# Root of the latents' mean squares on ScalarE (logarithm, exponential) instead of two POOL instructions

## The chip, the cores and the metric

One core of one Trainium2 chip runs the kernel. The metric is the time of one execution on the device in microseconds (us). A profiled execution gives the trace; there the engines are called PE (matrix multiply; its weight loads are PEld), DVE (vector), ACT (ScalarE, activation functions), POOL (GpSimd) and SP (DMA issue).

## The reference, cut to what matters

The reference is a trunk of two layers over 1024 tokens of width 1024. Each layer normalises the input, projects it, runs four branches A to D side by side, gates each, and projects the concatenation back. The change sits in branch D, the latent attention. Its queries and keys come from two normalised latents:

```
def rms_norm(x, g, eps=NORM_EPS):
    y = xf * lax.rsqrt(jnp.mean(jnp.square(xf), axis=-1, keepdims=True) + eps)
q  = (rms_norm(cq,  qa_g)  @ qb_w)     # cq: 256 wide
kv = (rms_norm(ckv, kva_g) @ kvb_w)    # ckv: 128 wide
```

Per token two factors are needed, 1/sqrt(mean(cq^2) + eps) and 1/sqrt(mean(ckv^2) + eps). Branch A, at work at the same time, ends in layer norm, SiLU and a pointwise matrix.

## The kernel before, in words

The tokens are cut into 8 tiles of 128, taken from tile 7 down to tile 0. Each stage of a layer is a Python generator: `th_a` to `th_atail` for branch A, `th_b`, `th_c`, `th_d` and `keys` for the latents, `th_att` for the attention itself, `th_w` for the loads of the output weights, `gate_f` for the gates. `weave` draws from them by the due times in `PLAN`, and this gives a program order. Tile's planner (`schedule_with_timeline_sim=True`, L1183) then orders each engine's queue with a timeline of its own: of the instructions of an engine that are ready in it, the one that stands first in the program goes first. So a queue need not follow the program, and at run time each engine takes its queue strictly in order.

Per tile, `th_d` multiplies by the split weights into `psd` (L209 to L211, 24 matmuls), copies the 384 latents to `cn` (ACT, L824), squares and sums them on ACT (`jd`, L827 and L828, with the sums in `ms`, 128x2), takes the root (L829), makes the queries' factor `rq` (DVE, L830), transposes `cn` on PE (L832) and copies the parts out (`ckT`, `cqT`). `keys`, one tile later, multiplies `ckT` (`pk`, L847), scales it by `ms` on ACT (`kk` and `vD`, L850 and L851), transposes (L860) and copies into `kT`. `psd`, `pk` and the attention's `psc` share two PSUM buffers.

There are two helpers for the root. `rstd_p` (L145) uses two POOL instructions, an addition of eps (L146) and a power of -0.5 (L147); it is used for A, B, C and D. `rstd` (L141) uses two on ACT: a logarithm with eps as bias (L142) and an exponential with scale -0.5 (L143); it is used for the norms of the residual stream.

ACT evaluates a function only with its table in place. `pin_tables` (L1089) runs after the planner and puts a load of the one table that has both Exp and Ln ahead of an Exp or Ln where the last function from a table was another (L1103); loads for Silu and Sigmoid are put in ahead of the instruction that needs them and carry its line. Copy and Square need no load of their own. In the stretch of the latents, Exp comes from branch C (`lm`, L738) and from the attention (`pe`, L933), and Silu from the gates (L353) and from branch A (`hsA`, L507): two `hsA` instructions (m = 0 and 1) for each half of the tokens, whose input `pt2A` are transposes on PE (L506), and whose output is used by the pointwise matmuls `pyA` (L515).

Of the kernel before, what the change touches and what calls it, by code (L numbers as in the profile page):

```python
# [99 lines left out]
def trunk_kernel(ctx, tc, x, pos, pre_g, post_g, wd, wv, w256, wo, cols, rows, pw, qb, kvb,  # L100
# [11 lines left out]
    def big(name):  # L112
        return pbig.tile([P, 1024], F32, tag="big", name=name)
# [27 lines left out]
    def rstd(out_, ms, e=0):  # L141
        A.activation(out_, ms, AF.Ln, bias=eps[:, e:e + 1])  # L142
        A.activation(out_, out_, AF.Exp, scale=-0.5)  # L143

    def rstd_p(out_, ms, e=0):  # L145
        G.tensor_tensor(out_, ms, eps[:, e:e + 1].to_broadcast(list(ms.shape)), op=ALU.add)  # L146
        G.tensor_tensor(out_, out_, mhalf.to_broadcast(list(ms.shape)), op=ALU.pow)  # L147
# [11 lines left out]
    def copy(name, out_, in_):  # L159
        (V.tensor_copy if name in ONV else A.copy)(out_, in_)  # L160
# [17 lines left out]
    def load_chunk(l, which, idx=0, spare=None):  # L178

        hs, ls = [], []  # L180
        if which == "d":
            parts, kk, n = 4, 2, ND
        elif which == "v":
            parts, kk, n = 2, 4, NV
        else:
            parts, kk, n = 2, 4, 256
        for q in range(parts):
            src = wd[l, q] if which == "d" else wv[l, q] if which == "v" else w256[l, idx, q]
            raw = wst.tile([P, kk, n], F32, tag="raw", name="raw", bufs=NRAW)
            nc.sync.dma_start(out=raw, in_=src)  # L190
            if spare is not None and q == parts - 1:
                h = spare.tile([P, kk, n], F32R, tag="k4", name="wh4", bufs=NK4)
                lo = spare.tile([P, kk, n], F32R, tag="k4", name="wl4", bufs=NK4)
            else:
                h = wst.tile([P, kk, n], F32R, tag="wh", name="wh", bufs=NWH)
                lo = wst.tile([P, kk, n], F32R, tag="wl", name="wl", bufs=NWL)
            split("wh", h, lo, raw)
            for k in range(kk):
                hs.append(h[:, k, :])
                ls.append(lo[:, k, :])  # L200
        return hs, ls

    def proj_tok(hT, hs, ls, i, n, ps):

        hh, hl = hT
        for k in range(KD):
            a = hh[:, k, i * P:(i + 1) * P]
            b = hl[:, k, i * P:(i + 1) * P]
            T.matmul(ps[:, :n], a, hs[k], start=(k == 0), stop=False)  # L209
            T.matmul(ps[:, :n], a, ls[k], start=False, stop=False)  # L210
            T.matmul(ps[:, :n], b, hs[k], start=False, stop=(k == KD - 1))  # L211
# [67 lines left out]
    for l in range(L):  # L279
# [16 lines left out]
        def blk(name, n=512, shape=None, parts=P):  # L296
            return shaped(br.tile([parts, n], F32, tag="blk", name=name, bufs=NBLK, padded_shape=[P, 544]), shape)
# [4 lines left out]
        def tmp(n, name, shape=None, parts=P):  # L302
            tag, cap, nb = ("t1k", 256, NT1) if n <= 256 else ("t15", 384, NT15) if n <= 384 else ("t2k", 512, NT2)
            return shaped(br.tile([parts, n], F32, tag=tag, name=name, bufs=nb, padded_shape=[P, cap]), shape)

        def small(n, name, bufs=2, shape=None):
            return shaped(br.tile([P, n], F32, tag=name, name=name, bufs=bufs), shape)
# [489 lines left out]
        def th_d():  # L797
            nc.gpsimd.dma_start(out=qbt, in_=qb[l])
            nc.gpsimd.dma_start(out=kvt, in_=kvb[l])
            for kb in range(2):  # L800
                V.tensor_scalar(qbt[:, kb, :], qbt[:, kb, :], col[:, C_QAG + kb:C_QAG + kb + 1], None, op0=ALU.mult)
            V.tensor_scalar(kvt, kvt, col[:, C_KVG:C_KVG + 1], None, op0=ALU.mult)
            hs, ls = load_chunk(l, "d", spare=br)
            vts, behind = {}, None
            for i in ORDER:
                g = i // 4
                if (0, g) not in kT:
                    for h in range(4):
                        kT[h, g] = blk("kT", parts=100)

                        nc.gpsimd.dma_start(out=kT[h, g][96:100, :], in_=amask[0])
                    for c in range(2):
                        cqT[c, g] = blk("cqT")
                if i // 2 not in vts:
                    vts[i // 2] = blk("vD", 512, (P, 8, 64))
                vD[i] = vts[i // 2][:, (i % 2) * 4:(i % 2) * 4 + 4, :]
                csl = slice((i % 4) * P, (i % 4 + 1) * P)
                pd_ = big("psd")
                ps, pt = pd_[:, 0:512], pd_[:, 512:1024]
                proj_tok(hT, hs, ls, i, ND, ps)  # L820
                ms = small(2, "msd", 3)
                cn = tmp(384, "cn")
                jd = br.tile([P, 384], BF16, tag="jd", name="jd", bufs=1)
                copy("cn", cn, ps[:, 0:384])  # L824
                krd = small(32, "krd", 3, (P, 2, 16))
                copy("krd", krd.rearrange("p a j -> p (a j)"), ps[:, 384:416])
                A.activation(jd[:, 0:256], cn[:, 0:256], AF.Square, scale=1.0 / 16, accum_out=ms[:, 0:1])  # L827
                A.activation(jd[:, 256:384], cn[:, 256:384], AF.Square, scale=128.0 ** -0.5, accum_out=ms[:, 1:2])  # L828
                rstd_p(ms, ms)  # L829
                V.tensor_scalar(rq[:, i:i + 1], ms[:, 0:1], SCALE, None, op0=ALU.mult)  # L830
                for c in range(3):
                    T.transpose(pt[:, c * P:(c + 1) * P], cn[:, c * P:(c + 1) * P], idn)  # L832
                ckT = small(P, "ckT", 3)
                copy("ckT", ckT, pt[:, 256:384])
                for c in range(2):
                    copy(f"cqT{c}", cqT[c, g][:, csl], pt[:, c * P:(c + 1) * P])
                yield 6
                if behind is not None:
                    yield from keys(*behind)
                behind = (i, ckT, ms, krd)  # L840
            yield from keys(*behind)

        def keys(i, ckT, ms, krd):
            g, csl = i // 4, slice((i % 4) * P, (i % 4 + 1) * P)
            pk_ = big("pk")
            pk, ptk = pk_[:, 0:512], pk_[:, 512:1024]
            T.matmul(pk, ckT, kvt, start=True, stop=True)  # L847
            pkv = pk.rearrange("p (h d) -> p h d", h=4)
            kk = tmp(384, "kk", (P, 4, 96))
            scaled("kk", kk[:, :, 0:64], pkv[:, :, 0:64], ms[:, 1:2])  # L850
            scaled("vD", vD[i], pkv[:, :, 64:128], ms[:, 1:2])  # L851
            k1, k2 = small(32, "kr1", 2, (P, 2, 16)), small(32, "kr2", 2, (P, 2, 16))
            V.tensor_tensor(k1, krd, cosT[:, i], op=ALU.mult)
            for a in range(2):
                V.tensor_tensor(k2[:, a, :], krd[:, 1 - a, :], sinT[:, i, a, :], op=ALU.mult)
            V.tensor_tensor(k1, k1, k2, op=ALU.add)
            V.tensor_copy(kk[:, :, 64:96],
                          k1.rearrange("p a j -> p (a j)").unsqueeze(1).to_broadcast([P, 4, 32]))
            for h in range(4):
                T.transpose(ptk[0:96, h * P:(h + 1) * P], kk[:, h, :], idn)  # L860
            for h in range(4):
                copy(f"kT{h}", kT[h, g][0:96, csl], ptk[0:96, h * P:(h + 1) * P])
            yield 3
# [160 lines left out]
        def plan(name):  # L1024
# [5 lines left out]
            (islice(conv, plan("ca")[2]), plan("ca")), (conv, plan("cb")), (gate(7, 1), plan("gb")), (th_b(), plan("b")),  # L1030
            (gate_f(8, 0), plan("ga")), (gate_f(9, 1), plan("gd")), (gate(10, 2), plan("gc")),
            (th_x(), plan("x")), *([(th_rot(), plan("rot"))] if l == 0 else []), (th_atail(), plan("at")), (th_c(), plan("c")), (th_d(), plan("d")),
            (th_q0(), plan("q")))]
        weave(ths, plan("d")[1] + 0.5)
# [154 lines left out]
```

## Time and profile before

| | us |
|---|---|
| median of 3 runs (lowest to highest) | 1258.37 (1258.11 to 1260.59) |
| profiled execution, its own time | 1256.95 |
| its span, first to last instruction | 1255.2 |
| PE busy | 1196.8 (95% of the span) |
| DVE busy | 808.7 (64%) |
| ACT busy | 488.5 (39%) |
| POOL busy | 180.0 (14%) |

A busy PE is one with a matmul under way. An engine's busy time leaves out the issue of DMAs and semaphores. A row of a timeline gives an instruction's start, its duration, engine, line, operation, output and input, count, and in brackets the idle time before it and what ended that.

### The profile page before, as it was taken

To read this page: it belongs to the slowest core of one execution; us is meant where nothing else is said; L and a number is where in the kernel's file an instruction comes from. 1 tells how busy PE (TensorE), PEld (TensorE's weight loads), DVE (VectorE), ACT (ScalarE), POOL (GpSimd) and SP (SyncE) were. 2 spreads that over 40 slices of the span, in tenths; PEclk is the share of its full clock that TensorE was granted. 3 is DMA by queue.
4 is the path that set the end of the run, shared out by engine and by line. 5 is a ranking of instruction groups with operands and counts; after the bars stand their busy time and mean duration, and the time that the engine had idled before them with its cause. 6 is when DMAs were issued, how large, how long until landed. Compare 5 with 4: busy or idle time off the path is not lost.

```text
span 1255.2 us, 17851 instructions
## 1 busy us (share of the span) xinstructions
PE 1196.8 (95%) x6902; PEld 985.2 (78%) x6902; DVE 808.7 (64%) x1555; ACT 488.5 (39%) x1112; POOL 180.0 (14%) x290
## 2 busy tenths in 40 slices
PE   5999999999989989999999999998999898999997
PEld 5988899888878846677898889897888696567786
DVE  5566999985366575527454859999763775654432
ACT  5413222233456474425432222322344755643311
POOL 2100011101132111211020001211011232011100
PEclk9999999999989999999999999998999999999999
DMA  8002122211142140234321111211013312111532
GB/s 275 34 34 68 43 85 79 71 41 52 54 134 74 40 154 19 73 125 168 104 94 68 34 51 60 86 59 67 34 49 101 118 60 100 49 40 43 176 138 81
DMA packets 38661, 101.48 MB, mean 81 GB/s; under 512 B 5440, under 2 KB 13808, under 8 KB 38576
## 3 DMA queue, kind: packets, MB, share of 16 engines
q1 hardware_dynamic: 22848, 51.42, 12.1%
q0 software_dynamic: 14864, 46.04, 11.0%
q10 hardware_dynamic: 864, 2.88, 0.6%
q8 instruction: 54, 0.88, 0.3%
q14 instruction: 31, 0.25, 0.1%
HBM read 75.37 MB, written 25.20 MB: 80 GB/s over the span
## 4 chain that ended last, share of the span: by engine, by line
PE 76%; DVE 11%; issue 4%; DMA 4%; ACT 3%; POOL 0%; SPq 0%; DVEq 0%; ACTq 0%; POOLq 0%
PE pz L1012 11%; PE psx L220 4%; PE psx L223 4%; PE psx L226 4%; DVE ca L481 3%; PE poD L949 3%; PE psc L926 3%; PE ptp L944 2%; PE plB L625 2%; PE psA L220 2%; PE psA L223 2%; PE psA L226 2%; PE psgA L347 2%; PE psgA L348 2%; PE psgA L349 2%
## 5 line engine op out<-in xcount | busy, mean ns | idle before, releaser
L481 DVE SCALAR_TENSOR_TENSOR ca<-hpad,col,ca 128x512 f32<-128x512 f32 x240 | 186.1, 781 | 4.0
L176 DVE TENSOR_TENSOR wl<-raw,wh 128x1024 fp32r<-128x1024 f32 (+2 forms) x56 | 66.9, 1194 | 95.3 <-ACT wh L160 95.2
L160 ACT CAST wh<-raw 128x1024 fp32r<-128x1024 f32 (+2 forms) x56 | 57.5, 1027 | 141.5 <-PE psA L223 33.7
L1012 PE MATMUL pz<-woh,yh 128*128 128x512 f32 x240 | 76.9, 400 | 1.2 <-ACT yh L160 1.2
L1012 PE MATMUL pz<-woh,yl 128*128 128x512 f32 x240 | 76.6, 398 | 0.2 <-DVE yl L176 0.2
L1012 PE MATMUL pz<-wol,yh 128*128 128x512 f32 x240 | 76.0, 396 | 0.0
L209 PE MATMUL psg<-wh,hh 128*128 128x256 f32 x256 | 73.9, 289 | 1.5 <-ACT gt L160 1.4
L210 PE MATMUL psg<-wl,hh 128*128 128x256 f32 x256 | 73.2, 286 | 0.0
L211 PE MATMUL psg<-wh,hl 128*128 128x256 f32 x256 | 72.8, 284 | 0.0
L625 PE MATMUL plB<-qz,krb 128*128 128x128 f32 x448 | 62.8, 288 | 8.6 <-DVE krb L635 8.6
L625 PEld LDWEIGHTS plB<-qz,krb 128*128 128x128 f32 x448 | 58.0, 199 | 11.0 <-issue 5.1
L933 ACT ACTIVATE pe<-psc,nm 128x1024 f32<-128x1024 f32 (+7 forms) x64 | 47.1, 738 | 42.6 <-DVE nm L928 22.4
L220 PE MATMUL psx<-hh,wh 128*128 128x512 f32 x192 | 62.8, 406 | 0.0
L223 PE MATMUL psx<-hl,wh 128*128 128x512 f32 x192 | 62.2, 403 | 0.0
L226 PE MATMUL psx<-hh,wl 128*128 128x512 f32 x192 | 61.9, 401 | 0.0
L719 DVE SCALAR_TENSOR_TENSOR xbc<-xpad,col,xbc 128x512 f32<-128x512 f32 x72 | 51.1, 748 | 16.3 <-ACT xbc L172 15.5
L926 PE MATMUL psc<-kT,qTt 96*128 96x512 f32 (+4 forms) x128 | 53.4, 544 | 5.7 <-ACT pe L933 3.5
L1012 PEld LDWEIGHTS pz<-wol,yh 128*128 128x128 f32 x240 | 44.9, 188 | 10.3
L1012 PEld LDWEIGHTS pz<-woh,yl 128*128 128x128 f32 x240 | 44.7, 188 | 10.4 <-DVE yl L176 0.6
L1012 PEld LDWEIGHTS pz<-woh,yh 128*128 128x128 f32 x240 | 44.1, 188 | 10.7 <-ACT yh L160 1.4
L348 PE MATMUL psgA<-hl,wh 128*128 128x512 f32 x128 | 51.0, 398 | 0.0
L347 PE MATMUL psgA<-hh,wh 128*128 128x512 f32 x128 | 50.9, 397 | 0.0
(335 smaller groups left out, 3001.2 us busy)
## 6 DMA issues: line engine op xcount, KB each, us to landing
raw<-in_w_dram SPq DMA_DIRECT2D x44, 512.0 KB, 3.4
rawo<-in_wo_dram SPq DMA_DIRECT2D x16, 512.0 KB, 3.5
gsp<-gt POOLq DMA_DIRECT2D x16, 256.0 KB, 2.5
gl<-gsp POOLq DMA_DIRECT2D x8, 512.0 KB, 5.1
gspF<-gtA POOLq DMA_DIRECT2D x16, 256.0 KB, 2.3
ysp<-gl POOLq DMA_DIRECT2D x8, 512.0 KB, 3.4
lm<-acsp POOLq DMA_DIRECT2D x16, 256.0 KB, 4.0
yt<-ysp SPq DMA_DIRECT2D x16, 256.0 KB, 3.4
```

What stands on the lines that cost most here:

```text
L209: T.matmul(ps[:, :n], a, hs[k], start=(k == 0), stop=False)
L210: T.matmul(ps[:, :n], a, ls[k], start=False, stop=False)
L211: T.matmul(ps[:, :n], b, hs[k], start=False, stop=(k == KD - 1))
L220: T.matmul(ps[:, h * 512:(h + 1) * 512], w, hh[:, k, h * 512:(h + 1) * 512], start=(k == 0), stop=False)
L223: T.matmul(ps[:, h * 512:(h + 1) * 512], w, hl[:, k, h * 512:(h + 1) * 512], start=False, stop=False)
L226: T.matmul(ps[:, h * 512:(h + 1) * 512], wl, hh[:, k, h * 512:(h + 1) * 512], start=False, stop=(k == KD - 1))
L347: T.matmul(ps, w, hh[:, k, tk], start=(k == 0), stop=False)
L348: T.matmul(ps, w, hl[:, k, tk], start=False, stop=False)
L481: V.scalar_tensor_tensor(t, hp[:, k:k + 512], w[k], t, op0=ALU.mult, op1=ALU.add)
L625: T.matmul(pl[:, o0:o0 + P].rearrange("p (r b u) -> p r b u", r=2, u=u), k_[:, t_ * P:(t_ + 1) * P], z[:, :, t_ * P:(t_ + 1) * P].rearrang ...
L926: T.matmul(psc[:, c0:c1_], qTt[0:k_, 2 * m + r, :], kT[2 * m + r, c0 // 512][0:k_, 0:c1_ - c0], start=True, stop=True)
L1012: T.matmul(pz[n], a[:, k, :], w[:, k, n * 512:(n + 1) * 512], start=(k == 0 and a is yh and w is wh), stop=(k == KD - 1 and a is yl))
```

## The change

In `th_d` the root of the two mean squares is taken by `rstd` instead of `rstd_p`. Eight tiles in two layers make 16 places. Nothing else in the source differs.

```
                 A.activation(jd[:, 256:384], cn[:, 256:384], AF.Square, scale=128.0 ** -0.5, accum_out=ms[:, 1:2])
-                rstd_p(ms, ms)
+                rstd(ms, ms)
                 V.tensor_scalar(rq[:, i:i + 1], ms[:, 0:1], SCALE, None, op0=ALU.mult)

     def rstd(out_, ms, e=0):
         A.activation(out_, ms, AF.Ln, bias=eps[:, e:e + 1])
         A.activation(out_, out_, AF.Exp, scale=-0.5)

     def rstd_p(out_, ms, e=0):
         G.tensor_tensor(out_, ms, eps[:, e:e + 1].to_broadcast(list(ms.shape)), op=ALU.add)
         G.tensor_tensor(out_, out_, mhalf.to_broadcast(list(ms.shape)), op=ALU.pow)
```

## Rows read from the trace of the kernel before

**Rows 1.** Busy time by stretch: bounds, length, PE, PEld, DVE, ACT, POOL, PEclk, DMA, GB/s.

```profile
355.00:450.00 95.00, 87.20 (x486) 71.73 (x484) 63.00 (x201) 56.54 (x182) 26.32 (x43) 0.96 0.27 89
971.00:1068.00 97.00, 88.54 (x493) 71.47 (x492) 64.79 (x205) 57.45 (x183) 26.82 (x44) 0.97 0.30 97
```

**Rows 2.** Instructions of lines 146 and 147 (ns min/median/max), and who waited.

```profile
L146 POOL TENSOR_TENSOR msd<-msd,eps x16: 186/194/649, 361.5 to 1055.6; 128x2 f32<-128x2 f32 x16
...
L147 POOL TENSOR_TENSOR msd<-msd,mhalf x16: 692/711/760, 361.8 to 1056.3; 128x2 f32<-128x2 f32 x16
...
  DVE rq L830: 4.0, 6
```

**Rows 3.** Instructions of lines 142 and 143, the same columns.

```profile
L142 ACT ACTIVATE ss<-ss,eps x16: 294/296/316, 7.1 to 642.8; 128x1 f32<-128x1 f32 x16
...
L143 ACT ACTIVATE ss<-ss x16: 193/203/213, 7.4 to 643.2; 128x1 f32<-128x1 f32 x16
```

**Rows 4.** Timeline of ACT at tile 2's root and branch A's second half, layer 0.

```profile
414.71 0.19 ACT L828 ACTIVATION_READ_ACCUMULATOR jd<-cn 128x1 f32 x1
414.92 1.28 ACT L507 ACT_TABLE_LOAD   x1
416.21 1.45 ACT L507 ACTIVATE hsA<-pt2A,col 128x512 f32<-128x512 f32 x2
```

**Rows 5.** Timeline of PE in the same stretch.

```profile
414.44 0.82 PE L506 MATMUL pt2A<-idn,hnA 128*128 128x128 f32 x6
...
417.71 1.98 PE L515 MATMUL pyA<-hsA,pwt 128*128 128x512 f32 x4
419.53 1.02 PE L847 MATMUL pk<-kvt,ckT 128*128 128x512 f32 x2
```

**Rows 6.** Timeline of ACT at the same place in layer 1.

```profile
1030.98 0.19 ACT L828 ACTIVATION_READ_ACCUMULATOR jd<-cn 128x1 f32 x1
1031.18 1.28 ACT L507 ACT_TABLE_LOAD   x1
```

**Rows 7.** Timeline of ACT in layer 0's first norm: the same helper beside other work.

```profile
17.21 0.18 ACT L233 ACTIVATION_READ_ACCUMULATOR hn<-xt 128x1 f32 x1
17.30 0.56 ACT L160 CAST hh<-pst 128x512 fp32r<-128x512 f32 x1
17.76 0.29 ACT L142 ACTIVATE ss<-ss,eps 128x1 f32<-128x1 f32 x1
17.96 0.57 ACT L160 CAST hh<-pst 128x512 fp32r<-128x512 f32 x1
18.43 0.20 ACT L143 ACTIVATE ss<-ss 128x1 f32<-128x1 f32 x1
```

**Rows 8.** Timeline of ACT at tile 1, layer 0.

```profile
429.56 0.27 ACT L160 COPY cqT<-psd 128x128 f32<-128x128 f32 x1 [2.72 <-DVE ckT L160]
```

**Rows 9.** Timelines of DVE and ACT where the attention starts, layer 0, then layer 1.

```profile
448.13 1.21 DVE L928 TENSOR_REDUCE nm<-psc 128x1 f32<-128x1024 f32 x1
448.94 1.28 ACT L1103 ACT_TABLE_LOAD   x1
1066.44 1.23 DVE L928 TENSOR_REDUCE nm<-psc 128x1 f32<-128x1024 f32 x1
1067.77 1.28 ACT L1103 ACT_TABLE_LOAD   x1
```

**Rows 10.** Timeline of PE there: last keys and first scores, layer 0, then layer 1.

```profile
446.33 3.25 PE L926 MATMUL psc<-kT,qTt 96*128 96x512 f32 x6 [0.97 <-ACT kT L160]
1060.88 0.64 PE L860 MATMUL pk<-idn,kk 128*96 128x128 f32 x4 [1.58 <-ACT vD L166]
1062.63 6.59 PE L926 MATMUL psc<-kT,qTt 100*128 100x512 f32 x8 [1.10 <-ACT kT L160]
1070.32 1.99 PE L926 MATMUL psc<-kT,qTt 100*128 100x512 f32 x4 [1.11 <-ACT pe L933]
```

**Rows 11.** Busy time by stretch, columns as in Rows 1.

```profile
370.00:372.00 2.00, 1.22 (x7) 1.19 (x6) 2.00 (x7) 1.13 (x4) 0.06 (x1) 0.50 0.00 0
```

More of the change, by code (lines that the diff above doesn't have):

```diff
@@ L828, in th_d @@
                 A.activation(jd[:, 256:384], cn[:, 256:384], AF.Square, scale=128.0 ** -0.5, accum_out=ms[:, 1:2])
-                rstd_p(ms, ms)
+                rstd(ms, ms)
                 V.tensor_scalar(rq[:, i:i + 1], ms[:, 0:1], SCALE, None, op0=ALU.mult)
```

## The prediction

> **What bounds the kernel now.** I read the split by stretch first, then the two lines that go, then the timelines of each engine around them. The places of the change lie in two stretches, one in each layer, where PE is busy for 87.2 of 95 and 88.5 of 97 us [rows 1]. So PE sets the pace, with some 8 us of idle time in each, and ACT, at 57 us, is far from full. What the change is worth is read from the few places where PE waits for ACT, DVE or the shared buffers. The two POOL instructions take 0.19 and 0.71 us [rows 2]. The only engine that is seen waiting for them is DVE, at `rq`, 6 times of 16 and 4.0 us together [rows 2], and DVE is not the engine that sets the pace.
>
> **What goes.** 16 x (0.19 + 0.71) = 14.4 us of POOL [rows 2]. POOL has nothing urgent queued behind them: it is busy for 26 of 95 us [rows 1], and the DMA issues that stand behind one in its queue are not what PE waits for. I count 0 for it by itself; the most it could give is the 4.0 us of DVE's waits, below.
>
> **What comes.** Logarithm and exponential take 0.30 and 0.20 us on a 128x1 tile [rows 3]; for 128x2, which the trace doesn't show, I take the same. That is 0.5 us on ACT per tile, 8 us in all. From the end of the sums to the factor it is about 0.5 us in place of 0.9 and two hand-overs, so `rq` comes 0.4 to 0.5 us sooner. At best the 4.0 us of DVE's waits shrink by 6 x 0.5 = 3 us, and only a part of that would reach PE. At worst each of the 16 pairs pushes a copy for which PE waits: 8 us. Both sit in queues with slack (DVE 63 and ACT 57 of 95 us [rows 1]), and the two have opposite signs. I take 0 and keep -2 and +2 for the range.
>
> **What the change does to the tables is the larger term.** A table load takes 1.28 us and the next ACT instruction starts 1.29 us after it [rows 4]. Three things have to be followed.
>
> First, the table with both functions is in place at tiles 7 to 3, since branch C's exponentials keep it there. At tile 2 the sums end at 414.90 and the load for branch A's SiLU starts at 414.92 [rows 4]; in layer 1 the two stand at 1031.17 and 1031.18 [rows 6]. After that no exponential comes before the attention, where the other table is loaded at 448.94 and 1067.77 [rows 9]. With the root on ACT that load has to come earlier, at tile 2 or at tile 1. The count stays the same, and a wait at the attention's start goes. In layer 0 `pe` starts with the load's end at 450.23, while its maximum was ready at 448.13 + 1.21 = 449.34: 0.9 us less the hand-over, 0.8. In layer 1 the maximum was there at 1067.67 and ACT free at 1067.75, so `pe` could start 1.3 us earlier; PE, which waits 1.11 us for it [rows 10], gets 1.1. Together -1.9 us. At its new place, tile 1, the load lies beside an idle time of ACT: between 426.84 and 429.56, right behind tile 1's sums, ACT stands idle for 2.72 us [rows 8], and load, logarithm and exponential need 1.29 + 0.5 = 1.8. Cost there: 0. Without that cover it would be 1.8 per layer.
>
> Second, where the new pair falls against the two SiLU instructions of tile 2's neighbourhood. Each of the new instructions waits for the one before it on its own engine, and the planner fills such gaps with what is ready. The same helper in the first norm shows it: between the sum and the logarithm stands a cast, and another between logarithm and exponential [rows 7]. Of the 24 pairs in the first 60 us and from 545 to 645 us, 8 have an instruction between the two. At tile 2 the SiLU instructions are what is ready: their input, `pt2A`, is finished at 415.26 [rows 5], and in the queue of before they follow the sums directly. The new pair stands ahead of them in the program, but is ready only after the gap. So I expect SiLU 0, then the logarithm, then SiLU 1 ahead of or behind the exponential. Each change of function then needs its table. Against one load now there are three, and a fourth for what comes after, which is the one moved from the attention. SiLU 1 is late by one more load of each table, logarithm and exponential: 1.29 + 0.30 + 0.20 + 1.29 = 3.1 us.
>
> Third, who waits for SiLU 1. It ends at 416.21 + 1.45 = 417.66 and `pyA` starts at 417.71 [rows 4, 5]: no slack at all. Behind `pyA` in PE's queue stand `pk` and the next tile's 24 matmuls, for which PE has no other work. The full 3.1 us would be lost if the queue stays in its order and `pyA` waits for both halves. If its first matmul, which uses half 0 alone, runs ahead, it is 3.1 - 0.4 = 2.7, with 0.4 a quarter of `pyA`'s 1.82 (417.71 to the start of `pk` at 419.53). If the planner puts `pk` and the next tile ahead of `pyA`, only the 1.8 us that `pyA` filled are open. I take 2.7 and keep 1.8 and 3.1.
>
> In the same neighbourhood `rq` waits for the exponential and DVE's queue for `rq`; the buffers that `psd` needs hang on DVE's copies behind it. This lies beside the same wait of PE, so I count it once.
>
> **A rule of the skill.** A load and the instruction behind it are 1.29 us apart in this trace [rows 4]. The Trainium skill ("ScalarE: Activation LUTs", What ACT_TABLE_LOAD costs) puts a switch of set at about 2.66 us, with a drain of 1.38 us beside the load, and its rule in Table sets is to batch calls by set. By that price the two extra switches in each layer would cost 5.4 us more in all, and the time would be 1267. The trace shows no such second part, so the sum goes by 1.29.
>
> **The sum.** 2 x 2.7 - 1.9 + 0 = +3.5 us. Against the profiled execution's own time of 1256.95 us this gives 1260.5. That execution lies 1.4 us under the median of the runs shown, 1258.37, against which the change will be timed: 1258.37 + 3.5 = 1261.9. One term is left out: a stall of PE can lower its clock. Around 370 us, with PE busy for only 1.22 of 2 us, the granted clock is 0.50 (1.2 GHz) [rows 11], and in layer 1 the first 8 score matmuls take 6.59 us (0.82 each) where in layer 0 six take 3.25 (0.54) [rows 10]. A stall of 2.7 us could bring such a stretch in each layer, at 8 x (0.82 - 0.54) = 2.2 us. It is not certain, so it is in the range: up to +4.4.
>
> **Rivals.** Measured time can tell 0.2%, that is 2.5 us, from no change: below 1255.9 is faster, above 1260.9 slower.
>
> *The pair stays together.* The planner puts logarithm and exponential both ahead of, or both behind, the two SiLU instructions, or both SiLU instructions between them. Then no load is added and one is moved. Ahead, SiLU 1 is late by 0.5 us; the sum is 2 x 0.5 - 1.9 = -0.9, or 1257.5. For it: 16 of the 24 pairs stand together. Against it: in these other work was often not waiting, as it is here. It decides wherever nothing else is ready in the planner's time when the sums end.
>
> *One layer splits the pair and the other doesn't.* 2.7 + 0.5 - 1.9 = +1.3: 1259.7. Against it: both layers have the same order at this place [rows 4, 6].
>
> *Faster: the end of the latents in layer 1 comes in another order.* There the last `keys` sit behind a cast of output weights in ACT's queue, PE waits 1.58 us for `vD`, and runs the next 8 score matmuls at the low clock [rows 10]. With the root earlier the planner can put `kk` and `vD` ahead of that cast. If besides the pair stays together: -0.8 for layer 0's load, -1.6 and -2.2, that is 1253.8. It needs two orders to come out well. For it: in layer 0 the same place runs at 0.54 us per matmul.
>
> *Slower elsewhere.* The new durations reorder the same end in layer 0 as it now is in layer 1: +1.6 + 2.2 beside the pair that stays together, 1261.3.
>
> **How the numbers follow.** Split in both layers 0.42 (1261.9; its own range 1259 to 1267), pair together 0.30 (1257.5), one layer 0.10 (1259.7), faster order 0.13 (1253.8), slower order 0.05 (1261.3). The range 1254 to 1267 holds the split with one or two stretches at the low clock, both middle cases, and a good half of the faster one; some 2 in 10 lie outside. Slower by over 0.2%: 0.34 of the split, 0.02 of one layer, 0.02 of the pair, 0.04 of the last: 0.42. Faster: 0.12 of the faster order, 0.05 of the pair with its uncertainty of 2 us: 0.17. The rest, 0.41, is within 0.2%.
>
> **What would show it.** In ACT's timeline at tile 2 of each layer: two more loads between the sums and the second `hsA`, and `pyA` some 2.7 us late against the `psd` matmuls ahead of it. The table loads would rise by four in all. At the attention's start the load ahead of `pe` should be gone, and stand at tile 1. The `rq` waits of DVE on POOL would be gone, and new ones on ACT shorter, except at tile 2. The prediction fails if the count of loads stays, if `pyA` has moved behind other matmuls, or if the planner's order differs far from these places.

## The result, and the profile after

The changed kernel takes 1269.93 us (median of 6 runs, 1268.43 to 1272.79), the kernel before beside it 1258.98 (6 runs, 1256.89 to 1260.93). The ratio is 1.0089, with a 95% interval of 1.0073 to 1.0106: about 11 us slower. The forecast was 3.5 us slower, 1261.9, with a range of 1254 to 1267. So the sign was right and the size a third of what came; the time lies outside the range.

The profiled execution spans 1268.4 us, where that of before spans 1255.2. PE runs the same instructions in the same order, save some of the last output matmuls. ACT at tile 2 of layer 0, by its timeline (start, duration, engine, line, operation; in brackets the idle time ahead and what ended it), answers to [rows 4]:

```profile
413.02 0.19 ACT L828 ACTIVATION_READ_ACCUMULATOR jd<-cn 128x1 f32 x1
413.24 0.30 ACT L142 ACTIVATE msd<-msd,eps 128x2 f32<-128x2 f32 x1
413.56 1.28 ACT L507 ACT_TABLE_LOAD   x1
414.85 0.78 ACT L507 ACTIVATE hsA<-pt2A,col 128x512 f32<-128x512 f32 x1
415.65 1.28 ACT L1103 ACT_TABLE_LOAD   x1
416.94 0.20 ACT L143 ACTIVATE msd<-msd 128x2 f32<-128x2 f32 x1
417.17 1.28 ACT L507 ACT_TABLE_LOAD   x1
418.46 0.78 ACT L507 ACTIVATE hsA<-pt2A,col 128x512 f32<-128x512 f32 x1
```

The logarithm and the exponential stand on either side of SiLU 0, and three loads stand where one did. From the start of the last read of the sums to the end of the second `hsA` it takes 419.24 - 413.02 = 6.22 us; before, 417.66 - 414.71 = 2.95. So SiLU 1 is 3.27 us later. Layer 1 has the same order. The table loads rose from 23 to 27: 13 for logarithm and exponential and 6 for this SiLU, which were 11 and 4, by the groups of instructions (line, operation, count, busy us, mean ns, idle us ahead):

```profile
L1103 ACT ACT_TABLE_LOAD x13 | 16.7, 1283 | 1.9 <-PEq L1176 1.7
L507 ACT ACT_TABLE_LOAD x6 | 7.7, 1283 | 0.1
```

What PE makes of it, in both layers, by its timeline [rows 5 for before]:

```profile
415.19 0.60 PE L742 MATMUL ptx<-idn,xbc 128*128 128x128 f32 x4
417.81 0.68 PE L774 MATMUL pstC<-xdt,btk 128*128 128x128 f32 x4 [2.02 <-DVE xdt L771]
419.29 3.58 PE L515 MATMUL pyA<-hsA,pwt 128*128 128x512 f32 x4 [0.80 <-ACT hsA L507]
422.71 1.02 PE L847 MATMUL pk<-kvt,ckT 128*128 128x512 f32 x2
...
1042.72 0.68 PE L774 MATMUL pstC<-xdt,btk 128*128 128x128 f32 x4 [2.02 <-DVE xdt L771]
1044.20 3.45 PE L515 MATMUL pyA<-hsA,pwt 128*128 128x512 f32 x4 [0.80 <-ACT hsA L507]
```

Two things are to be seen. PE stands idle for 2.02 + 0.80 = 2.82 us. And then `pyA`'s four matmuls take 3.58 and 3.45 us, where they took 1.98 [rows 5]. The stretches of layer 0 (columns as in [rows 1]) show why: the granted clock, the third number from the end, falls to 0.50 (1.2 GHz) behind the idle time.

```profile
416.00:418.00 2.00, 0.19 (x2) 0.22 (x3) 0.82 (x4) 1.97 (x3) 0.00 (x0) 1.00 0.00 0
420.00:422.00 2.00, 2.00 (x3) 0.67 (x2) 1.38 (x5) 0.37 (x1) 0.58 (x1) 0.50 0.00 0
```

The same stretch of PE's queue can be measured in every profile of this study, because PE's order in it is the same: from the 2310th matmul (a `pyC` ahead of `pstC`; `pyC`, `pstC` and `xdt` are branch C's) to the 2330th (`pk`), in layer 1 from the 5760th (`pyC` too) to the 5785th (the next tile's first `psd`), starts of both. I call it the tile 2 stretch. It takes 3.97 and 5.08 us before, 8.78 and 9.76 after: 4.81 + 4.68 = 9.5 us of the 11.

DVE's `rq` waits for the exponential, and `xdt`, which `pstC` needs, is queued behind it:

```profile
417.18 0.15 DVE L830 TENSOR_SCALAR rq<-msd 128x1 f32<-128x1 f32 x1 [2.89 <-ACT msd L143]
417.25 0.41 DVE L771 TENSOR_TENSOR xdt<-xdt,wdec 128x256 f32<-128x256 f32 x1
```

At tile 1 the moved load stands ahead of the logarithm, behind the sums and two copies of `kT`, and at the attention's start (the last line) it is gone; this answers to [rows 8, 9]:

```profile
429.61 0.41 ACT L160 COPY kT<-pk 96x128 f32<-96x128 f32 x2
430.03 1.28 ACT L1103 ACT_TABLE_LOAD   x1
431.33 0.30 ACT L142 ACTIVATE msd<-msd,eps 128x2 f32<-128x2 f32 x1
...
452.95 1.11 ACT L933 ACTIVATE pe<-psc,nm 128x1024 f32<-128x1024 f32 x1 [0.49 <-DVE nm L928]
```

### The profile page after: what moved, and what is told of

Same layout as the page of the kernel before. It is cut to its first block, busy times and chain, and to the rows that moved or that the text cites. A ratio compares the mean times of both kernels' runs of the same rounds, so it can differ in the third digit from the quotient of the medians.

```text
span 1268.4 us, 17821 instructions
## 1 busy us (share of the span) xinstructions
PE 1203.4 (95%) x6902; PEld 990.3 (78%) x6902; DVE 809.5 (64%) x1555; ACT 499.4 (39%) x1148; POOL 164.8 (13%) x258
## 4 chain that ended last, share of the span: by engine, by line
PE 78%; DVE 10%; ACT 5%; DMA 3%; issue 2%; DVEq 0%; ACTq 0%
PE pz L1012 13%; PE psx L223 4%; PE psx L220 4%; PE psx L226 4%; PE poD L949 3%; DVE ca L481 3%; PE psc L926 3%; PE ptp L944 3%; PE plB L625 2%; PE psA L220 2%; PE psA L223 2%; PE psA L226 2%; PE psgA L347 2%; PE psgA L348 2%; PE psgA L349 2%
```

## The experiments

Three theories. A: what costs is that SiLU 1 is late by the two extra loads, as PE waits for it and then runs at the lower clock. B: what costs is DVE's queue behind `rq`. C: it is neither, but the 16 pairs in ACT's queue and the new order elsewhere. All runs were timed in 5 rounds against the kernel before; the brackets are 95% intervals, and the differences below are the ratio times that kernel's time.

**The two loads taken away.**

```
@@ tile loop, after
-                rstd(ms, ms)
+                (A.activation(ms, ms, AF.Identity, bias=eps[:, 0:1]), A.activation(ms, ms, AF.Identity, scale=-0.5)) if i == 2 else rstd(ms, ms)
```

> The changed kernel, but in the pass of tile 2 (both layers) the logarithm and the exponential are two Identity activations on the same 128x2 tile, which need no table; every queue keeps the order of the changed kernel, and the load that the change moved to tile 1 stays there. The query scale and the keys of tile 2 come out with other values. Only the two table loads between and behind the pair are gone, in each layer. Theory A (the SiLU instruction's lateness of one table load of each kind, some 3.3 us in each layer, is what PE waits for, directly and by the lower clock behind the stall) expects 1259 to 1262 us, 8 to 11 us under the changed kernel. Theory B (DVE's queue stuck behind rq) expects the same, since rq comes sooner too. Theory C (the 16 pairs spread over ACT's queue, or the other order of PE and DVE elsewhere) expects over 1266 us.

1261.78 us, ratio 1.0031 [1.0016, 1.0046]: 3.9 us over the kernel before, so some 7 of the 11 us are gone with two loads per layer. Theory C in its pure form falls. In the timeline of ACT the second `hsA` is late by no more than the two small instructions, and in that of PE `pyA` is back at full clock:

```profile
415.00 0.78 ACT L507 ACTIVATE hsA<-pt2A,col 128x512 f32<-128x512 f32 x1
415.67 0.19 ACT L829 ACTIVATE msd<-msd 128x2 f32<-128x2 f32 x1
415.76 0.77 ACT L507 ACTIVATE hsA<-pt2A,col 128x512 f32<-128x512 f32 x1
```

```profile
416.53 0.68 PE L774 MATMUL pstC<-xdt,btk 128*128 128x128 f32 x4 [0.59 <-ACT hsA L507]
417.05 1.88 PE L515 MATMUL pyA<-hsA,pwt 128*128 128x512 f32 x4
```

Here `pstC`, which reads nothing of `hsA`, waits for it. `pt2A`, `pstC` and `pyA` share one pair of PSUM buffers (the tag smA), so the likely reason is the buffer that SiLU 0 sets free; by the same turn of buffers the first `pyA` would need the one that SiLU 1 sets free. Neither was tried by itself.

**The two loads alone, in the kernel before.**

```
@@ pin_tables, before
+                if fn is AF.Silu and str(i.outs[0].memref).startswith("hsA"):
+                    hsa += 1
+                    if hsa % 4 == 3:
+                        nc.scalar.preload_act_table_set("natural_log_exp_and_others")
+                        b.instructions.insert(k + 1, end.pop())
+                        k += 1
```

> The kernel before, with POOL's root everywhere, and one edit: behind the first SiLU instruction of the second group in each layer the exponential's table is loaded, so that the second one needs its own table again. Two loads more in each layer, 2.58 us of ACT, and nothing else; rq waits for POOL as before. Theory A expects 2 x (2.6 to 4.5) us over the kernel before: 1264 to 1268. Theory B, for which rq must be late, expects less than 3 us over it: at most 1262. Theory C expects no more than 2 x 1.3 us over it.

1266.30 us, ratio 1.0061 [1.0046, 1.0076]: 7.7 us over the kernel before, with POOL's root and an `rq` that is not late. Theory A foretold it, theory B did not. The two layers of its profile show what each part of the price is:

```profile
414.02 0.61 PE L774 MATMUL pstC<-xdt,btk 128*128 128x128 f32 x4
417.18 1.98 PE L515 MATMUL pyA<-hsA,pwt 128*128 128x512 f32 x4 [2.55 <-ACT hsA L507]
...
1033.54 0.61 PE L774 MATMUL pstC<-xdt,btk 128*128 128x128 f32 x4
1036.70 3.66 PE L515 MATMUL pyA<-hsA,pwt 128*128 128x512 f32 x4 [2.55 <-ACT hsA L507]
```

The wait is 2.55 us in both. In layer 0 the clock stays and the tile 2 stretch is 2.71 us longer than before; in layer 1 the clock falls and it is 4.41 us longer.

**The pair kept together.**

```
@@ after
-        A.activation(out_, out_, AF.Exp, scale=-0.5)
+        return A.activation(out_, out_, AF.Exp, scale=-0.5)
...
+                    in_order([roots[2], hsi] if g == 1 and m == 0 else [])
...
-                rstd(ms, ms)
+                roots[i] = rstd(ms, ms)
```

> The changed kernel, with an order given to the planner alone (no wait on the chip): the first SiLU instruction of the second group stands behind tile 2's exponential. ACT then does logarithm, exponential, one load, SiLU, SiLU: 23 loads in all as before the change in place of 27. The rest of the change (16 pairs on ACT, no POOL root, the other place of the load of the attention) stays. Theories A and B expect 1257 to 1261 us, level with the kernel before or a little under it. Theory C expects over 1266 us.

1261.08 us, ratio 1.0020 [1.0007, 1.0033]: 2.5 us over the kernel before, just past the upper edge of what A and B expected. The order came out as asked:

```profile
410.96 0.30 ACT L142 ACTIVATE msd<-msd,eps 128x2 f32<-128x2 f32 x1
411.29 0.20 ACT L143 ACTIVATE msd<-msd 128x2 f32<-128x2 f32 x1
411.51 1.28 ACT L507 ACT_TABLE_LOAD   x1
412.81 1.45 ACT L507 ACTIVATE hsA<-pt2A,col 128x512 f32<-128x512 f32 x2
```

Its tile 2 stretches take 4.48 and 5.59 us, half a microsecond more than before in each layer, which is the pair itself. What it says of the change: one order of four instructions is worth some 8 us.

**`rq` taken out of DVE's queue.**

```
@@ tile loop, after
-                V.tensor_scalar(rq[:, i:i + 1], ms[:, 0:1], SCALE, None, op0=ALU.mult)
+                A.mul(rq[:, i:i + 1], ms[:, 0:1], SCALE) if i == 2 else V.tensor_scalar(rq[:, i:i + 1], ms[:, 0:1], SCALE, None, op0=ALU.mult)
```

> The changed kernel, with rq of tile 2 alone written by ACT in place of DVE (both layers). The loads stay (27), and the second SiLU instruction comes a little later still, by one small ACT instruction at most; DVE's queue no longer holds an instruction that waits for the exponential, so the matmul pstC should not wait for DVE's xdt. Theory A alone (PE waits for the SiLU either way, at pyA if not at pstC) expects 1268 to 1271 us. Theory B (the wait at pstC adds to that at pyA) expects 4 to 5 us under the changed kernel: some 1265. Theory C expects no change.

1268.73 us, ratio 1.0082 [1.0068, 1.0097]: 10.3 us over the kernel before, and the interval overlaps that of the change. Theory B falls. PE's wait has only moved:

```profile
416.88 0.71 PE L774 MATMUL pstC<-xdt,btk 128*128 128x128 f32 x4
420.49 1.98 PE L515 MATMUL pyA<-hsA,pwt 128*128 128x512 f32 x4 [2.90 <-ACT hsA L507]
...
1037.70 0.71 PE L774 MATMUL pstC<-xdt,btk 128*128 128x128 f32 x4
1041.31 3.78 PE L515 MATMUL pyA<-hsA,pwt 128*128 128x512 f32 x4 [2.89 <-ACT hsA L507]
```

2.90 us in one piece at `pyA` replace 2.02 + 0.80. And again the same idle time leaves the clock alone in layer 0 and halves it in layer 1: the tile 2 stretch is 3.21 us longer than before there, and 6.10 here.

**Tile 2 alone, and all but tile 2.** The next two split the change by tiles: with `rstd` for `i == 2` and `rstd_p` for the rest, and the other way round.

```
@@ tile loop, after
-                rstd(ms, ms)
+                (rstd if i == 2 else rstd_p)(ms, ms)
```

```
-                rstd(ms, ms)
+                (rstd_p if i == 2 else rstd)(ms, ms)
```

> The kernel before with ScalarE's logarithm and exponential for tile 2 alone (both layers) and POOL's root for the other 14 tiles: the two loads inside the SiLU pair are there, the queues elsewhere are those of the kernel before. If the two loads at tile 2 are worth what their removal gave (7 to 8 us) and the rest of the change the other 3 to 4, this is 7 to 8 us over the kernel before. If the loads alone carry all of the change, 10 to 11 us over it.

1268.20 us, ratio 1.0089 [1.0069, 1.0110]: 11.2 us over the kernel before. Two pairs of the 16 make the whole difference. Its tile 2 stretches take 8.78 and 11.00 us, and `pyA` runs at the lower clock in both layers (3.53 and 3.78 us). Against the two loads alone the stretches are 2.10 and 1.51 us longer (8.78 - 6.68 and 11.00 - 9.49): the pair's own half microsecond in each layer, and beside it more time at the lower clock.

> The changed kernel with POOL's two instructions again for tile 2 alone (both layers); the other 14 pairs are ScalarE's. PE's queue is that of the changed kernel. No table load is added inside the SiLU pair, and the pair of SiLU instructions is not late, not even by the 0.5 us of a logarithm and an exponential. If what the runs without the two loads keep (3 to 4 us over the kernel before) is the pair's own 0.5 to 0.7 us at tile 2 in each layer, this is 1.0 to 1.4 us faster than they: some 2 us over the kernel before. If it comes from the other 14 pairs and from the other order, it stays at 3 to 4 us over it.

1258.43 us, ratio 1.0010 [0.9994, 1.0026]: 1.3 us over the kernel before, no difference that can be told. The tile 2 stretches are those of before (3.92 and 5.03). So the other 14 pairs and the other order cost little by themselves, nearer to the first of the two readings (some 2 us) than to the second.

**What is left: all tables away.** Same queues as the change, no table function in any of the 16 pairs (the edit of the first experiment without its condition).

> The changed kernel, but all 16 pairs of logarithm and exponential are two Identity activations on the same tile, which need no table: every queue keeps the order of the changed kernel, there are 23 loads, and the one that was moved to tile 1 stands at the start of the attention again, as before the change. The factors of queries and keys come out with other values. Against the run in which only tile 2's pair is replaced (3.7 us over the kernel before) it differs by the moved load: if that load's price at tile 1 (0.8 to 0.9 us in each layer) and its gain at the attention (0.7 to 0.9) cancel, this is 3 to 4 us over the kernel before, and what is left comes from the queues and the 16 pairs; if the moved load is what is left, it is level with the kernel before.

1264.55 us, ratio 1.0045 [1.0030, 1.0060]: 5.7 us over the kernel before, more than either reading expected. That the moved load is what is left is refuted. With that load back at the attention the kernel is not faster but, if anything, slower by 1.8 us than the first experiment; their intervals overlap.

**The moved load by itself.** The first attempt named the copy `cn` among the ACTIVATE instructions, of which it is none; the load stayed where it was. So the next two runs are repeats, of the kernel before and of the pair kept together.

> The kernel before, with POOL's root everywhere, and one edit: the exponential's table, loaded at the start of the attention, is loaded ahead of tile 1's copy cn instead, where ACT stands idle for 3.1 us. 23 loads as before; this is the moved load of the change alone, at a place that costs nothing. If the load ahead of the attention's first exponential is worth what the prediction took (0.8 us in layer 0 and 1.1 in layer 1), the time is 1.4 to 1.9 us under the kernel before, and the start of the attention is shorter by that in the trace. If the load there was hidden, no difference.

1257.87 us, ratio 0.9997 [0.9984, 1.0011], as a repeat should.

> The changed kernel with tile 2's pair kept ahead of the two SiLU instructions (23 loads), and besides the load that stood at tile 1 between the sums and the logarithm is made earlier, ahead of tile 1's copy cn, where ACT stands idle for 3.1 us. The run with the pair together alone lay 2.5 us over the kernel before. If the load at tile 1, which delays the next tile's matmuls by 0.8 to 0.9 us in each layer, is what is left, this gives 1.6 to 1.8 us of it back: some 1 us over the kernel before. If the rest comes from the 16 pairs spread over ACT's queue or from the new order, it stays at 2 to 3 us over it.

1262.82 us, ratio 1.0031 [1.0015, 1.0047]: 3.9 us over the kernel before, where its twin had 2.5. The two intervals overlap.

> The kernel before, unchanged: a second profile of it, to see which differences between single profiles are those of the kernel (stretches at the low clock around 370 and 990 us above all). Every theory expects a ratio of 1.000 within 0.002; if the stretch at 990 us runs at the low clock here as it does in the changed kernel, that stretch is no effect of the change.

1257.72 us, ratio 1.0003 [0.9989, 1.0017]. This third profile of the same program (the attempt above gave the second) shows which stretches vary by themselves. The tile 2 stretch is 3.97 and 5.08 us in all three. The 40 matmuls from the 5490th, around 990 us, take 8.8 us before and in this profile, and 12.0 in the second one. Busy time by stretch, here and then in that second profile:

```profile
989.00:993.00 4.00, 4.00 (x23) 3.34 (x22) 2.43 (x9) 2.19 (x7) 1.62 (x3) 1.00 0.65 132
```

```profile
989.00:993.00 4.00, 4.00 (x17) 3.59 (x17) 2.89 (x9) 1.05 (x4) 2.09 (x3) 0.50 0.47 107
```

The granted clock is 1.00 in the one and 0.50 in the other, with the same program. That stretch takes 12.0 us in the profile of the change too, so its 3 us prove nothing about the change. Every profile of another kernel here has 10.2 to 12.1 us for it; with one or two profiles of each, whether some of what is left lies there stays open.

The second attempt:

```
@@ pin_tables, before; and the same in the kernel with the pair together
+                hsa += fn is AF.Silu and str(i.outs[0].memref).startswith("hsA")
+                if hsa and hsa % 4 == 0 and cur is AF.Silu and str(i.engine).endswith("Activation") and i.outs and str(getattr(i.outs[0], "memref", "")).startswith("cn"):
+                    nc.scalar.preload_act_table_set("natural_log_exp_and_others")
+                    b.instructions.insert(k, end.pop())
+                    k += 1
+                    cur = "both"
```

> The kernel before with one edit: the exponential's table is loaded ahead of tile 1's copy cn, where ACT stands idle for 3.1 us, and no longer at the start of the attention (the earlier attempt left the load where it was, and its run is a repeat of the kernel before). 23 loads. By the prediction's term: 0.8 us gained at the attention's start of layer 0 and 1.1 in layer 1, 1.4 to 1.9 us under the kernel before. A rival, from the traces of the runs so far: layer 1 gives nothing, because ACT's next instruction behind the first exponential is a cast of output weights that waits for its DMA; then at most 0.8 to 1 us.

1254.94 us, ratio 0.9979 [0.9968, 0.9989]: 2.6 us under the kernel before, and the one version here that beats both. ACT's timeline shows the load in the idle time, the same idle time behind it cut from 3.11 to 2.09 us, and `pe` at the attention's start waiting for its maximum and no longer for a table:

```profile
417.44 1.28 ACT L1103 ACT_TABLE_LOAD   x1
420.81 0.48 ACT L160 COPY cn<-psd 128x384 f32<-128x384 f32 x1 [2.09 <-PE psd L211]
...
444.64 1.11 ACT L933 ACTIVATE pe<-psc,nm 128x1024 f32<-128x1024 f32 x1 [0.55 <-DVE nm L928]
```

Where the 2.6 us lie is not settled. Counted from `pk` to `poD` (the table further down), the attention's start is 0.5 us shorter in layer 0 and 0.5 us longer in layer 1, so this profile shows no gain, both layers together, at the places that the load left. In layer 0 PE's wait for `pe` falls from 2.03 us (kernel before, repeated) to 1.06. In layer 1 the first 12 score matmuls, counted to the `ptp` behind them, take 8.24 us in place of 9.52 (1072.15 - 1062.63 in the kernel before), without the low clock of [rows 10]. But by `poD` that lead is lost: from the first of those matmuls to `poD` it is 15.76 us, and 15.12 before. There ACT's next instruction is a cast that waits for its weights:

```profile
1063.05 0.19 ACT L933 ACTIVATION_READ_ACCUMULATOR pe<-psc,nm 128x1 f32 x1
1064.39 1.15 ACT L976 ACTIVATE woh<-rawo,col 128x1024 fp32r<-128x1024 f32 x1 [1.14 <-DMA rawo<-in_wo_dram]
```

> The changed kernel with tile 2's pair ahead of the two SiLU instructions, and the load of tile 1 made ahead of tile 1's copy cn, in ACT's idle time (the earlier attempt left that load where it was, and its run is a repeat of the run with the pair together). If the load at tile 1 costs what the shift of the next tile's matmuls says at most (0.8 us in each layer), this lies 1.6 us under the run with the pair together, some 1.5 us over the kernel before. If the segment between tile 2 and tile 1, longer by 0.2 us in layer 0, is its whole price, no difference that can be measured: 3 us over the kernel before.

1260.45 us, ratio 1.0023 [1.0012, 1.0035]: 2.9 us over the kernel before. Its twins without the earlier load had 2.5 and 3.9, so the load at tile 1 has no price that these times can tell. In the traces it has a small one, 0.2 us in each layer (below), which is gone with the earlier load.

## Why the forecast had the sign and not the size

**What stands.** The order on ACT (SiLU 0 between logarithm and exponential, exponential ahead of SiLU 1), 27 loads in place of 23, the load gone from the attention and back at tile 1, PE's order kept: all as written. That the wait of `rq` lies beside the same wait of PE and counts once is shown by the run with `rq` on ACT. The price of a load was right as well: two of them make `pyA` wait 2.55 us where nothing else is late. By the Trainium skill's price ("ScalarE: Activation LUTs", What ACT_TABLE_LOAD costs: 2.66 us a switch) they would make it wait some 5.3, an estimate; no run here shows that. So the total of 1267 that the prediction worked out from that page was nearer to the result for a reason that isn't there.

**The step that failed first** is the one that reads "One term is left out: a stall of PE can lower its clock ... It is not certain, so it is in the range". The term 2 x 2.7 should have had it in the sum. `pyA` takes 3.58 and 3.45 us after, 1.98 before: 1.60 + 1.47 = 3.1 us. Over the four profiles with this stall (the change, tile 2 alone, the loads alone, `rq` on ACT) it happened in 6 of 8 places. I knew the price, from [rows 10], and wrote that a stall "could bring such a stretch" without taking a side; the 6 of 8 places say that most of this price belonged in the sum of the likeliest case. A place cost less than the 2.2 us that I had for it, 1.6 and 1.5.

**The second is the 2.7 itself.** I took 0.4 off the 3.1 because the first matmul of `pyA`, which uses half 0 alone, could run ahead. It did not in any run: all four start behind the second `hsA`, even where half 0 was done 3.4 us before (the loads alone). The full bound was right: PE's idle time is 2.82 us in place of none, and the stretch without the clock's part is 4.81 - 1.60 = 3.21 and 4.68 - 1.47 = 3.21 us longer. Twice 0.5 us is missing there.

**The third is the -1.9 for the moved load, layer 1's 1.1 us above all,** with the 0 for the 16 pairs and for the load at tile 1. All but tile 2 together measure +1.3, not -1.9. Counted by matmuls as in the tile 2 stretch, in us:

| stretch of PE's queue | before | the change | all but tile 2 | moved load alone |
|---|---|---|---|---|
| layer 0, behind tile 2 (2330th to 2430th) | 20.16 | 20.38 | 20.38 | 20.18 |
| layer 0, attention's start (2430th, `pk`, to 2480th, `poD`) | 19.36 | 18.99 | 18.49 | 18.89 |
| layer 1, behind tile 2 (5785th to 5880th) | 19.56 | 19.76 | 19.75 | 19.54 |
| layer 1, attention's start (5880th, `pk`, to 5935th, `poD`) | 21.24 | 21.91 | 21.87 | 21.74 |
| start of the last output projection (6500th to 6580th) | 16.30 | 16.90 | 16.89 | 17.08 |

In layer 0 the attention's start is 0.4 us shorter, and 0.9 in all but tile 2, about the 0.8 that I forecast (19.36 us in two profiles of the kernel before, 20.31 in the third). In layer 1, where I forecast 1.1 us less, it is 0.7 us longer; the three profiles of the kernel before agree there within 0.02 us. PE's and ACT's rows there, the first line from before, the others after the change, show where the time goes:

```profile
1072.58 1.89 PE L926 MATMUL psc<-kT,qTt 100*128 100x512 f32 x4
...
1074.37 5.40 PE L926 MATMUL psc<-kT,qTt 100*128 100x512 f32 x8 [1.68 <-ACT kT L160]
1085.12 1.99 PE L926 MATMUL psc<-kT,qTt 100*128 100x512 f32 x4 [1.63 <-ACT pe L933]
1082.82 1.15 ACT L976 ACTIVATE woh<-rawo,col 128x1024 fp32r<-128x1024 f32 x1 [1.81 <-DMA rawo<-in_wo_dram]
1083.88 1.10 ACT L933 ACTIVATE pe<-psc,nm 128x1024 f32<-128x1024 f32 x1
```

PE waits 1.68 us for the last `kT`, 1.10 before [rows 10], and then 1.63 us for the second `pe`, for which it had no wait before (first line). That `pe` stands behind a cast of output weights that waits 1.81 us for its DMA. So I took PE's wait of 1.11 us as a gain and did not look at what ACT has queued behind the first `pe`. That is not the whole cause: in the runs with the two loads alone and with tile 2 alone, where the load stays at the attention, this stretch is longer too (23.80 and 23.20 us), and why stays open.

The load at tile 1 shows as 0.2 us in each layer. The start of the output projection is 0.6 us longer with the new order of its matmuls; it is 17.1 us in two runs with the old order as well (the loads alone, the moved load alone), so the order need not be the reason. And `rq` waits longer, not shorter, as I had said it would: before, 4.0 us in 6 places [rows 2]; after, 11.2 us in 7, and with POOL at tile 2 still 5.5 in 5. What of this reaches PE outside tile 2 was not tried.

**The sum again**, from this case's profiles: 4.81 + 4.68 = 9.5 for the two tile 2 stretches, and by the table 0.22 - 0.37 + 0.20 + 0.67 + 0.60 = 1.3 for the rest, 10.8 together. The change measured 11. Of the 7.3 us between this and the forecast's 3.5, the clock is 3.1, the 2.7 taken too small 1.0, and the rest 3.2. One thing doesn't fit: the moved load alone measured -2.6 us, and by the table it would be 0.8 us slower; so single profiles don't carry differences of 2 to 3 us between whole kernels, and where those lie stays open, as for the runs that replace or tie the pair (2.5 to 5.7 us over the kernel before).

**The chances.** The likeliest case was the right one, at 0.42, with 1259 to 1267 as its own range. Its upper end had two stretches at the lower clock in it (+4.4), but set against gains that did not come. Two slips in the working change nothing here: four switches at 1.37 us more are 5.5, not 5.4, and the faster order leaves out the 2 x 0.5 us of the pair, with which it would be 1254.8.

## What to carry to other kernels

Two instructions that share a table are one unit only if nothing stands between them: where a planner fills gaps, look at what is ready in that gap, and if it needs another table, tie the pair together by an order. Price a new wait of PE by its length and by the matmuls behind it at half clock, and put that in the sum when the wait is as long as others that lowered the clock. A table load that sits on the path can be moved into an idle time of its engine by itself, without the change it came with; here the kernel with that alone was 2.6 us faster, though its trace doesn't show where. Before counting a wait as a gain, look at what the engine has queued behind it.

## What was not expected of the hardware

The same idle time of PE has two prices. With 2.90 us of idle time the granted clock stayed at 1.00 in layer 0 of the run with `rq` on ACT; with 2.89 us in layer 1 it fell:

```profile
422.00:424.00 2.00, 2.00 (x9) 1.28 (x8) 1.65 (x4) 1.00 (x3) 0.58 (x1) 1.00 0.08 5
...
1042.00:1044.00 2.00, 2.00 (x3) 0.68 (x2) 1.48 (x5) 0.37 (x1) 0.00 (x0) 0.50 0.03 8
```

The difference is 2.9 us on the tile 2 stretch. The Trainium skill ("TensorE: Matmul & The Clock Gate", HAM oscillation) says that work behind a wait can start at the lower clock; layer 1 agrees, and layer 0 shows that it need not. In the kernel before, the low clock around 990 us came and went between profiles of one program, so a single profile can't be used to price such a stretch.
